# Streaming the high and low token parts of the MLP's first product in one pass

## The chip, the cores and the metric

The kernel runs on one core of a Trainium2 chip. The metric is the device time of one execution in microseconds (us), as the median over runs. The engines are TensorE (PE, with its weight load PEld as a row of its own), VectorE (DVE), ScalarE (ACT), GpSimd (POOL) and SyncE (SP), which issues nearly all the DMAs.

## The reference

A trunk of two decoder layers works on 256 tokens of width 1024 in float32. In each layer one input projection feeds two attention mixers, an output projection adds their result to the residual stream, and a squared-ReLU MLP of width 4096 follows:

```python
for l in range(DEPTH):                       # DEPTH = 2
    h = _rms_norm(x, attn_norm[l])
    proj = h @ w_in[l]                       # 1024 -> 1720
    ...                                      # two attention groups on the same h
    x = x + mixed @ w_out[l]
    h = _rms_norm(x, mlp_norm[l])
    x = x + jnp.square(jax.nn.relu(h @ w_ff1[l])) @ w_ff2[l]     # 1024 -> 4096 -> 1024
return _rms_norm(x, final_norm)
```

## The kernel before

Every large product is made of three reduced-precision ones. An operand is split into a high part (the value rounded to the type float32r) and a low part (what is left), and `mm3` (lines 349 to 354) issues high by high (line 352), high by low (line 353) and low by high (line 354) into one accumulator. Low by low is left out.

**Weights** come from DRAM in the order of use, two chunks of 128 rows by 512 columns at a time (a "tile" here). `ask` (lines 314 to 340) issues the load, then two ScalarE casts make the high part (`whi`, line 334) and two subtractions make the low part (`wlo`, line 336). The engine of the subtractions is given by `lo_eng` (line 312): VectorE for the first two tiles and then for the tiles with an odd number in the layer, GpSimd for the others. Six raw and six split buffers exist, and four tiles are asked for ahead of the one in use.

**Tokens** of a layer are normalised by `norm` (line 417): VectorE multiplies by the gain, TensorE transposes four blocks, and `split_into` (line 389) writes the high part with one ScalarE copy and the low part with one VectorE subtraction, each 512 wide.

**The MLP** of a layer runs in four quarters of 1024 features. In a quarter, `up` (line 1060) is called twice (`fb` = 0 and 1) for 512 features each; features stand on the partitions and the 256 tokens stream. A call does two halves of 256 features. A half goes over the 8 chunks of the contraction and, in each, over two blocks of 128 features (`j`); for each of these pairs `mm3` issues three matmuls of 256 columns, with three weight loads. Both blocks of a half share one PSUM bank of the kind `acc`. When a half is done, `squared_relu` (line 1046) takes the bank to SBUF: relu and square on ScalarE give the high part of `u`, square and subtract on VectorE the low part. Then `down` (line 1082) is called twice (`nb` = 0 and 1) with `u` as the stationary operand and 512 columns of weights streaming, three matmuls for each of 8 chunks and two token tiles. For `nb` = 0 it takes the first four chunks of both token tiles first (they need only the `u` of `fb` = 0), then chunks 4 to 7, which need that of `fb` = 1. For the first `up` of a layer the halves alternate after four chunks, since the second four wait for the later half of the normalised tokens.

**PSUM** has 8 banks, named by kind: `acc` 2, `s` 3, `tr` 2, `pv` 1. Outside the MLP, `s` and `pv` serve the attention, and `s` the first projection of layer 0.

**Order of the work.** TensorE and SP run in the order in which the program's generators are stepped by `Driver`, a planner with a clock of its own; `dr.put` and `dr.event` give it the times at which a bank or a result is taken to be there. The order on VectorE, ScalarE and GpSimd is set by the scheduler of the tile framework. Each engine executes its own list strictly in order.

**The start of the program.** Layer 0's first projection (`proj_both`, PSUM kind `s`) takes the first four tiles of weights, the second projection tiles 5 to 8. Both need the tokens in two halves of 512 features; the second half of the second token tile is the last to be split. Line 1171 makes a small bfloat16 copy of the causal mask (`maskb`) that the attention uses later.

Of the kernel before, what the change touches and what calls it, by code (L numbers as in the profile page):

```python
# [17 lines left out]
L = 2  # L18
# [208 lines left out]
def trunk(ctx: ExitStack, tc: tile.TileContext, x, wst, gains, pos, cw2, cst, out):  # L227
# [83 lines left out]
    def lo_eng():  # L311
        return "v" if at_w[1] <= 2 or at_w[1] % (len(PLAN) // L) % 2 == 1 else "g"
# [104 lines left out]
    def norm(t, nb, g, hT, tag):  # L417

        yield "event", ("x", t, tag, nb * 512)
        if hT[nb] is None:  # L420
            hT[nb] = halves_pair(f"h{nb}")
        h = tm.tile([P, 512], F32, name="h", tag="tm")
        n = slice(nb * 512, nb * 512 + 512)
        with urgent():
            nc.vector.tensor_mul(h, X[t][:, n], g[:, n])
        yield "pe", 0, 700
        c = slice(t * P, (t + 1) * P)
        yield from split_into([h[:, j * P : (j + 1) * P] for j in range(4)], *(x[:, :, c] for x in hT[nb]))
        dr.event(("h", t, tag, nb), 1105)
# [28 lines left out]
    def layer(l, hT):  # L458
# [487 lines left out]
        for ch, r in enumerate(weights(16)):  # L946
# [10 lines left out]
            yield "pe", 300, 0  # L957
# [89 lines left out]
        def squared_relu(acc, u, half):  # L1047

            r = tm.tile([P, 512], F32, name="relu", tag="tm")
            c = slice(half * 2, half * 2 + 2)  # L1050
            hi, lo = (x[:, c, :].rearrange("p c n -> p (c n)") for x in u)
            with urgent():
                nc.scalar.activation(r, acc, AF.Relu)  # L1053
                dr.put("acc", 750)
                nc.scalar.activation(hi, r, AF.Square)
                sq = tm.tile([P, 512], F32, name="sq", tag="tm")
                nc.vector.tensor_mul(sq, r, r)  # L1057
                nc.vector.tensor_sub(lo, sq, hi.bitcast(F32))

        def up(u, fb, first):  # L1060


            src, w, accs, fresh = weights(KC), [], [None, None], [True, True]
            for half, chunks in [(0, (0, 4)), (1, (0, 4)), (0, (4, 8)), (1, (4, 8))] if first else [(0, (0, 8)), (1, (0, 8))]:
                for c in range(*chunks):
# [5 lines left out]
                    if c == 0:  # L1071
                        yield "get", "acc"
                        accs[half] = PS("acc")
                    for j in range(2):
                        f = slice((half * 2 + j) * P, (half * 2 + j + 1) * P)
                        mm3(accs[half][:, j * S : (j + 1) * S], [x[:, f] for x in w[c]], [x[:, c % 4, :] for x in hM[c // 4]], c == 0 and j == 0, c == KC - 1, skip_group_check=True)
                    yield "pe", 6 * 119, 0
                if chunks[1] == KC:
                    squared_relu(accs[half], u[fb], half)
            ev("u", id(u), fb, after=2400)  # L1080
# [66 lines left out]
    def main():  # L1147
# [23 lines left out]
        nc.vector.tensor_copy(maskb, K("causal"))  # L1171
# [27 lines left out]
```

## Time and profile before

| | |
|---|---|
| median of 3 runs (lowest to highest) | 642.43 us (640.5 to 645.75) |
| the profiled execution's own time | 646.11 us |
| its span, first to last instruction | 644.3 us |
| mean granted clock of TensorE | 0.986 |
| busy: PE | 621.4 us, 96% of the span |
| busy: PEld | 548.3 us, 85% |
| busy: DVE | 420.4 us, 65% |
| busy: ACT | 354.6 us, 55% |
| busy: POOL | 300.4 us, 47% |
| DMA | 108.48 MB, mean 168 GB/s |
| chain that ended last | PE 85%, DVE 7%, ACT 4%, DMA 3%, issue 1% |

The profile shows one execution; its time is 3.7 us over the median of the runs. A matmul's busy time runs from its start to the end of its pipeline, and consecutive matmuls overlap, so that the rate of TensorE is read from the distance between starts. A granted clock of 1.00 is 2.4 GHz, 0.50 is 1.2 GHz. "Idle before" is the time in which an engine waited, with the instruction that released it.

### The profile page before, as it was taken

Reading aid. Unit: us, or ns where it says so; the run is one execution under the profiler, and the core shown is the slowest. Engines: PE = TensorE matmul, PEld = TensorE weight load, DVE = VectorE, ACT = ScalarE, POOL = GpSimd, SP = SyncE. Lnnn points to the kernel's source line nnn. Section 1 sums busy time; section 2 is a strip of 40 time slices with the busy share of each in tenths; the row PEclk is TensorE's granted clock in tenths of the full one; section 3 lists DMA queues with packets and bytes.
Section 4 is the critical chain, followed back from the end, with each engine's and each line's share of the span. In section 5 each row is a group of like instructions: output and inputs, shape, how many; then the busy total and the mean of one; then the engine's idle time right before and its main releaser. Section 6 shows DMA issues by size and latency. Waiting matters only on the chain.

```text
span 644.3 us, 10909 instructions
## 1 busy us (share of the span) xinstructions
PE 621.4 (96%) x4099; PEld 548.3 (85%) x4099; DVE 420.4 (65%) x665; ACT 354.6 (55%) x735; POOL 300.4 (47%) x298
## 2 busy tenths in 40 slices
PE   7899899999999999999999889999999999999995
PEld 4697688889889899899888768798998998998985
DVE  4797778675656647558677866866664673764662
ACT  5566667565535546355564475765663654554551
POOL 2675404344553645445466631244544554554351
PEclk8899999999999999999999898999999999999998
DMA  8756733155555655745644665114547565565601
GB/s 306 264 175 206 236 116 100 34 198 173 185 169 191 208 182 166 226 155 186 213 126 134 211 212 199 34 66 149 177 142 220 164 200 174 193 204 176 198 1 66
DMA packets 31732, 108.48 MB, mean 168 GB/s; under 512 B 3776, under 2 KB 4416, under 8 KB 31680
## 3 DMA queue, kind: packets, MB, share of 16 engines
q1 hardware_dynamic: 31392, 107.27, 50.8%
q8 instruction: 32, 0.52, 0.3%
q10 hardware_dynamic: 288, 0.52, 0.2%
q14 instruction: 20, 0.16, 0.1%
HBM read 106.73 MB, written 1.05 MB: 167 GB/s over the span
## 4 chain that ended last, share of the span: by engine, by line
PE 85%; DVE 7%; ACT 4%; DMA 3%; issue 1%; SPq 0%; POOL 0%; POOLq 0%; ACTq 0%
PE acc L352 24%; PE acc L354 24%; PE acc L353 24%; PE tr L384 4%; DVE wlo L336 2%; PE pv L708 2%; DMA raw<-in_wst_dram 2%; PE pv L759 2%; ACT whi L334 1%; PE acc L949 1%; PE s L693 1%; DMA x<-in_x_dram 1%; PE s L746 1%; ACT p L646 1%; DVE qmT L233 1%
## 5 line engine op out<-in xcount | busy, mean ns | idle before, releaser
L336 POOL TENSOR_TENSOR wlo<-raw,whi 128x512 fp32r<-128x512 f32 (+3 forms) x178 | 245.0, 1397 | 221.2 <-ACT whi L334 220.9
L334 ACT CAST whi<-raw 128x512 fp32r<-128x512 f32 (+2 forms) x360 | 201.4, 610 | 113.6 <-PE acc L354 74.7
L336 DVE TENSOR_TENSOR wlo<-raw,whi 128x512 fp32r<-128x512 f32 (+3 forms) x182 | 170.5, 973 | 58.4 <-ACT whi L334 58.3
L352 PE MATMUL acc<-h,whi 128*128 128x256 f32 x512 | 145.3, 284 | 0.0
L354 PE MATMUL acc<-h,wlo 128*128 128x256 f32 x512 | 145.0, 283 | 0.0
L353 PE MATMUL acc<-h,whi 128*128 128x256 f32 x512 | 145.0, 283 | 0.0
L352 PE MATMUL acc<-whi,u 128*128 128x512 f32 (+1 forms) x264 | 101.5, 384 | 0.0
L353 PE MATMUL acc<-wlo,u 128*128 128x512 f32 (+1 forms) x264 | 101.2, 383 | 0.0
L354 PE MATMUL acc<-whi,u 128*128 128x512 f32 (+1 forms) x264 | 101.1, 383 | 0.0
L352 PEld LDWEIGHTS acc<-h,whi 128*128 128x128 f32 x512 | 98.3, 192 | 0.2
L353 PEld LDWEIGHTS acc<-h,whi 128*128 128x128 f32 x512 | 98.3, 192 | 0.2
L354 PEld LDWEIGHTS acc<-h,wlo 128*128 128x128 f32 x512 | 98.3, 192 | 0.0
L1057 DVE TENSOR_TENSOR sq<-relu 128x512 f32<-128x512 f32 x32 | 37.2, 1161 | 38.9 <-ACT relu L1053 38.9
L354 PEld LDWEIGHTS acc<-whi,u 128*128 128x128 f32 x264 | 49.6, 188 | 9.8
L353 PEld LDWEIGHTS acc<-wlo,u 128*128 128x128 f32 x264 | 49.7, 188 | 9.4
L352 PEld LDWEIGHTS acc<-whi,u 128*128 128x128 f32 x264 | 49.7, 188 | 9.3
L1029 DVE SCALAR_TENSOR_TENSOR x<-acc,r,x 128x512 f32<-128x512 f32 (+1 forms) x33 | 24.1, 731 | 49.0 <-PE acc L354 49.0
L1053 ACT ACTIVATE relu<-acc 128x512 f32<-128x512 f32 x32 | 19.0, 594 | 59.3 <-PE acc L354 59.3
L352 PE MATMUL acc<-whi,h 128*128 128x512 f32 (+2 forms) x112 | 41.2, 368 | 0.0
L353 PE MATMUL acc<-wlo,h 128*128 128x512 f32 (+2 forms) x112 | 40.2, 359 | 0.2 <-POOL wlo L336 0.2
L354 PE MATMUL acc<-whi,h 128*128 128x512 f32 (+2 forms) x112 | 39.9, 357 | 0.0
L646 ACT ACTIVATE p<-s,nm 128x128 f32<-128x128 f32 (+1 forms) x96 | 33.9, 430 | 7.9 <-DVE nm L640 4.0
(185 smaller groups left out, 913.3 us busy)
## 6 DMA issues: line engine op xcount, KB each, us to landing
raw<-in_wst_dram SPq DMA_DIRECT2D x178, 512.0 KB, 4.2
raw<-in_wst_dram SPq DMA_DIRECT2D x8, 416.0 KB, 3.3
raw<-in_wst_dram SPq DMA_DIRECT2D x4, 420.0 KB, 3.3
raw<-in_wst_dram SPq DMA_DIRECT2D x4, 384.0 KB, 3.1
x<-in_x_dram SPq DMA_DIRECT2D x4, 256.0 KB, 6.3
g_mix<-in_gains_dram SPq DMA_DIRECT2D x2, 512.0 KB, 5.8
g_mlp<-in_gains_dram SPq DMA_DIRECT2D x2, 512.0 KB, 5.1
g_attn<-in_gains_dram SPq DMA_DIRECT2D x2, 512.0 KB, 3.9
```

The source lines that it names most:

```text
L334: nc.scalar.copy(hi[:, v], r[:, v])
L336: E(eng).tensor_sub(lo[:, v], r[:, v], hi[:, v].bitcast(F32))
L352: mm(acc, ah, wh, start=start, stop=False, **k)
L353: mm(acc, ah, wl, start=False, stop=False, **k)
L354: mm(acc, al, wh, start=False, stop=stop, **k)
L384: nc.tensor.transpose(tr[:rows, c, :], col, ident)
L646: nc.scalar.activation(p[:, k], s[:, k], AF.Exp, bias=nm[:, a : a + 1], scale=scale)
L708: mm(o[:, a, br, :], pts[a // per][:, ((a % per) * 2 + br) * nk + kt, :], V[:, kt, br, g, :], start=kt == 0, stop=kt == nk - 1)
L759: mm(o[:, r, :], pts[r // per][:, (r % per) * nk + kt, :], VM[:, kt, hb * 4 + r, :], start=kt == 0, stop=kt == nk - 1)
L1029: nc.vector.scalar_tensor_tensor(X[t][:, c], acc, scale, X[t][:, c], op0=OP.mult, op1=OP.add)
L1053: nc.scalar.activation(r, acc, AF.Relu)
L1057: nc.vector.tensor_mul(sq, r, r)
```

## The change

In the MLP the normalised tokens are stored as chunk by (high, low) by 256 tokens, so that a chunk's high and low parts lie side by side. For each pair of chunk and feature block, `up` now issues two matmuls: the weights' high part with 512 columns (tokens high and low), which fill a whole bank, and the weights' low part with the 256 high columns, added to the first half of that bank. So each block of 128 features has a bank of its own; a half takes two, (`s`, `s`) for the first half and (`s`, `pv`) for the second. `squared_relu` first adds the two halves of each bank: ScalarE copies columns 256 to 511 to SBUF, VectorE adds columns 0 to 255 to them; then one VectorE instruction gives max(r, 0) times r, ScalarE copies that as the high part of `u`, and VectorE subtracts for the low part. `norm` writes the MLP's tokens with two ScalarE copies and two VectorE subtractions of 256 each instead of one and one of 512. The planner's times are changed with it.

Apart from the MLP, the low parts of the first eight tiles of weights of layer 0 (not only the first two) are made on VectorE, and `maskb` is copied by ScalarE instead of VectorE. One further edit puts a `yield` under `if True:` and does nothing; it is left out here.

```diff
     def lo_eng():
-        return "v" if at_w[1] <= 2 or at_w[1] % (len(PLAN) // L) % 2 == 1 else "g"
+        return "v" if at_w[1] <= 8 or at_w[1] % (len(PLAN) // L) % 2 == 1 else "g"
...
     def norm(t, nb, g, hT, tag):
...
-        if hT[nb] is None:
+        if tag[1] == "mlp":
+            if hT[nb] is None:
+                hT[nb] = [hl.tile([P, 2, 2, S], F32R, name=f"hm{nb}{i}", tag="hl") for i in range(2)]
+        elif hT[nb] is None:
             hT[nb] = halves_pair(f"h{nb}")
...
-        yield from split_into([h[:, j * P : (j + 1) * P] for j in range(4)], *(x[:, :, c] for x in hT[nb]))
+        cols = [h[:, j * P : (j + 1) * P] for j in range(4)]
+        if tag[1] == "mlp":
+
+            tr = yield from trans(cols)
+            with urgent():
+                for i, x in enumerate(hT[nb]):
+                    nc.scalar.copy(x[:, :, 0, c], tr[:, 2 * i : 2 * i + 2, :])
+                    nc.vector.tensor_sub(x[:, :, 1, c], tr[:, 2 * i : 2 * i + 2, :], x[:, :, 0, c].bitcast(F32))
+            dr.put("tr", 1050)
+        else:
+            yield from split_into(cols, *(x[:, :, c] for x in hT[nb]))
...
-        def squared_relu(acc, u, half):
+        def squared_relu(banks, kinds, u, half):
+
 
             r = tm.tile([P, 512], F32, name="relu", tag="tm")
+            low = tm.tile([P, 512], F32, name="sq", tag="tm")
             c = slice(half * 2, half * 2 + 2)
             hi, lo = (x[:, c, :].rearrange("p c n -> p (c n)") for x in u)
             with urgent():
-                nc.scalar.activation(r, acc, AF.Relu)
-                dr.put("acc", 750)
-                nc.scalar.activation(hi, r, AF.Square)
-                sq = tm.tile([P, 512], F32, name="sq", tag="tm")
-                nc.vector.tensor_mul(sq, r, r)
+                for j, acc in enumerate(banks):
+                    n = slice(j * S, (j + 1) * S)
+                    nc.scalar.copy(low[:, n], acc[:, S:])
+                    nc.vector.tensor_add(r[:, n], acc[:, :S], low[:, n])
+                    dr.put(kinds[j], 1000 + 400 * j)
+                sq = low
+                nc.vector.scalar_tensor_tensor(sq, r, 0.0, r, op0=OP.max, op1=OP.mult)
+                nc.scalar.copy(hi, sq)
                 nc.vector.tensor_sub(lo, sq, hi.bitcast(F32))
...
         def up(u, fb, first):
...
+                kinds = (("s", "s"), ("s", "pv"))[half]
...
-                        yield "get", "acc"
-                        accs[half] = PS("acc")
+                        accs[half] = []
+                        for kind in kinds:
+                            yield "get", kind
+                            accs[half].append(PS(kind))
+                    h = hM[c // 4][c % 4 // 2][:, c % 2]
                     for j in range(2):
                         f = slice((half * 2 + j) * P, (half * 2 + j + 1) * P)
-                        mm3(accs[half][:, j * S : (j + 1) * S], [x[:, f] for x in w[c]], [x[:, c % 4, :] for x in hM[c // 4]], c == 0 and j == 0, c == KC - 1, skip_group_check=True)
-                    yield "pe", 6 * 119, 0
+                        wh, wl = w[c]
+                        mm(accs[half][j], wh[:, f], h.rearrange("p k n -> p (k n)"), start=c == 0, stop=False)
+                        mm(accs[half][j][:, :S], wl[:, f], h[:, 0], start=False, stop=c == KC - 1)
+                    yield "pe", 2 * (227 + 120), 0
                 if chunks[1] == KC:
-                    squared_relu(accs[half], u[fb], half)
-            ev("u", id(u), fb, after=2400)
+                    squared_relu(accs[half], kinds, u[fb], half)
+            ev("u", id(u), fb, after=2900)
...
-        nc.vector.tensor_copy(maskb, K("causal"))
+        nc.scalar.copy(maskb, K("causal"))
```

How the lists of the engines move is shown at three places.

On VectorE near the start of the program, before (h is the tokens' low part, wlo the weights'):

```order
L394 TENSOR_TENSOR h_242<-tr,h_241 128x4x128
L336 TENSOR_TENSOR wlo<-raw,whi 128x512 x2
L1171 CAST maskb<-cs 128x128
L394 TENSOR_TENSOR h_242<-tr,h_241 128x4x128
L336 TENSOR_TENSOR wlo<-raw,whi 128x512
L446 SCALAR_TENSOR_TENSOR ra<-s,rx,cs 128x128
```

And with the change:

```order
L394 TENSOR_TENSOR h_242<-tr,h_241 128x4x128
L336 TENSOR_TENSOR wlo<-raw,whi 128x512 x4
L394 TENSOR_TENSOR h_242<-tr,h_241 128x4x128
L336 TENSOR_TENSOR wlo<-raw,whi 128x512 x3
L459 SCALAR_TENSOR_TENSOR ra<-s,rx,cs 128x128
L462 SCALAR_TENSOR_TENSOR rb<-s,rx,cs 128x2x32 x2
L336 TENSOR_TENSOR wlo<-raw,whi 128x512
```

Between the two subtractions of the tokens there are now four subtractions for weights where there were two and the mask; three more follow where there was one, and GpSimd's list loses its first six subtractions.

On TensorE in the MLP's first product, a pair of chunk and feature block and the transposes of the last token half, before (h_1710 holds the tokens' high part, h_1711 their low part):

```order
L352 MATMUL acc<-h_1710,whi 128x256
L353 MATMUL acc<-h_1711,whi 128x256
L354 MATMUL acc<-h_1710,wlo 128x256
L384 MATMUL tr<-idt,h 128x128 x4
L352 MATMUL acc<-h_1710,whi 128x256
```

And with the change (hm is the tile that holds high and low tokens):

```order
L1100 MATMUL s<-hm_1710,whi 128x512
L1101 MATMUL s<-hm_1710,wlo 128x256
L1100 MATMUL pv<-hm_1710,whi 128x512
L1101 MATMUL pv<-hm_1710,wlo 128x256
L384 MATMUL tr<-idt,h 128x128 x4
```

A pair has gone from three matmuls of 256 columns to one of 512 and one of 256, and each of the two pairs shown writes a bank of its own. The transposes of the last token half, which stood behind 24 matmuls of the first `up`, now stand behind 20, which are ten pairs instead of eight.

On VectorE at the end of a quarter's second `up`, before (first and second half, then the weights for `down`):

```order
L1057 TENSOR_TENSOR sq<-relu 128x512
L1058 TENSOR_TENSOR u_2281<-sq,u_2280 128x512
L336 TENSOR_TENSOR wlo<-raw,whi 128x512 x4
L1057 TENSOR_TENSOR sq<-relu 128x512
L1058 TENSOR_TENSOR u_2281<-sq,u_2280 128x512
L336 TENSOR_TENSOR wlo<-raw,whi 128x512 x2
```

And with the change:

```order
L1072 TENSOR_TENSOR relu<-s,sq 128x256 x2
L1075 SCALAR_TENSOR_TENSOR sq<-relu 128x512
L336 TENSOR_TENSOR wlo<-raw,whi 128x512 x2
L1077 TENSOR_TENSOR u_2241<-sq,u_2240 128x512
L336 TENSOR_TENSOR wlo<-raw,whi 128x512 x2
L1072 TENSOR_TENSOR relu<-s,sq 128x256
L1072 TENSOR_TENSOR relu<-pv,sq 128x256
L1075 SCALAR_TENSOR_TENSOR sq<-relu 128x512
L1077 TENSOR_TENSOR u_2241<-sq,u_2240 128x512
L336 TENSOR_TENSOR wlo<-raw,whi 128x512 x2
```

On ScalarE at the same place, before and then with the change:

```order
L1053 ACTIVATE relu<-acc 128x512
L1055 ACTIVATE u_2280<-relu 128x512
L334 CAST whi<-raw 128x512 x8
L1053 ACTIVATE relu<-acc 128x512
L1055 ACTIVATE u_2280<-relu 128x512
L334 CAST whi<-raw 128x512 x16
```

```order
L1071 COPY sq<-s 128x256 x2
L334 CAST whi<-raw 128x512 x2
L1076 CAST u_2240<-sq 128x512
L334 CAST whi<-raw 128x512 x4
L1071 COPY sq<-s 128x256
L334 CAST whi<-raw 128x512 x2
L1071 COPY sq<-pv 128x256
L1076 CAST u_2240<-sq 128x512
L334 CAST whi<-raw 128x512 x16
```

Two additions have come in on VectorE for each half, and the subtraction of the weights' tiles stays where it was for the last half. On ScalarE the last of the four tiles' casts now stands between the two copies of the last half; the number of casts ahead of its end is the same, eight.

## Rows read from the trace of the kernel before

**Rows 1.** Windows by stage: busy time of each engine (instructions), then granted clock, DMA

```profile
28.00:58.00 30.00, 28.73 (x165) 25.73 (x163) 27.28 (x57) 16.86 (x43) 21.45 (x28) 1.00 0.59 193
...
180.00:250.00 70.00, 70.00 (x465) 64.72 (x464) 41.29 (x42) 34.48 (x60) 34.92 (x26) 1.00 0.57 185
```

**Rows 2.** Groups by line: the high-by-low matmuls of the first product

```profile
L353 PE MATMUL acc<-h,whi 128*128 128x256 f32 x512 | 145.0, 283 | 0.0
```

**Rows 3.** Timeline of PE in a quarter: start, us; second product first and last, first product

```profile
167.02 0.40 PE L352 MATMUL acc<-whi,u 128*128 128x512 f32 x1
...
188.58 0.39 PE L354 MATMUL acc<-whi,u 128*128 128x512 f32 x1
188.81 0.28 PE L352 MATMUL acc<-h,whi 128*128 128x256 f32 x1
...
211.72 0.28 PE L354 MATMUL acc<-h,wlo 128*128 128x256 f32 x1
```

**Rows 4.** Lines with 256-wide reads of PSUM on DVE and ACT: min/median/max ns

```profile
L496 DVE TENSOR_TENSOR kT<-tr,kT x8: 406/417/425, 37.0 to 365.1; 128x256 fp32r<-128x256 f32 x8
...
L501 ACT COPY kcT<-tr x4: 362/376/378, 35.9 to 344.7; 128x256 f32<-128x256 f32 x4
```

**Rows 5.** Timeline of DVE at the start of the program

```profile
18.34 2.55 DVE L336 TENSOR_TENSOR wlo<-raw,whi 128x512 fp32r<-128x512 f32 x2 [0.86 <-ACT whi L334]
20.82 1.28 DVE L1171 CAST maskb<-cs 128x128 bf16<-128x128 f32 x1
22.02 0.68 DVE L394 TENSOR_TENSOR h<-tr,h 128x512 fp32r<-128x512 f32 x1
...
26.81 0.35 DVE L446 SCALAR_TENSOR_TENSOR ra<-s,rx,cs 128x128 f32<-128x128 f32 x1 [3.01 <-PE s L354]
```

**Rows 6.** Timelines of ACT and POOL at the same time

```profile
16.65 2.18 ACT L334 CAST whi<-raw 128x512 fp32r<-128x512 f32 x4
18.73 0.58 ACT L393 CAST h<-tr 128x512 fp32r<-128x512 f32 x1
...
17.36 8.82 POOL L336 TENSOR_TENSOR wlo<-raw,whi 128x512 fp32r<-128x512 f32 x6 [0.88 <-ACT whi L334]
```

**Rows 7.** Timeline of PE at the same time, and its next wait

```profile
19.71 0.40 PE L353 MATMUL s<-wlo,h 128*128 128x512 f32 x1
22.76 0.80 PE L354 MATMUL s<-whi,h 128*128 128x512 f32 x1 [2.65 <-DVE h L394]
...
25.84 0.39 PE L352 MATMUL s<-whi,h 128*128 128x512 f32 x1
...
53.78 0.44 PE L384 MATMUL tr<-idt,kd 128*128 128x128 f32 x2 [1.27 <-DVE qT L530]
```

**Rows 8.** Windows behind these two waits (columns as in the first group)

```profile
22.70:25.50 2.80, 2.74 (x7) 2.17 (x8) 1.10 (x1) 0.00 (x0) 2.80 (x3) 0.50 0.96 340
...
53.80:57.00 3.20, 3.20 (x18) 3.15 (x19) 2.21 (x7) 1.54 (x5) 2.29 (x5) 1.00 0.82 270
```

**Rows 9.** Timelines of DVE, ACT and PE at the end of a quarter's first product

```profile
166.31 3.46 DVE L336 TENSOR_TENSOR wlo<-raw,whi 128x512 fp32r<-128x512 f32 x2 [1.53 <-ACT whi L334]
169.69 1.77 DVE L1057 TENSOR_TENSOR sq<-relu 128x512 f32<-128x512 f32 x1
171.57 0.69 DVE L1058 TENSOR_TENSOR u<-sq,u 128x512 fp32r<-128x512 f32 x1
...
167.14 1.14 ACT L334 CAST whi<-raw 128x512 fp32r<-128x512 f32 x2 [0.34 <-issue]
...
174.30 0.39 PE L354 MATMUL acc<-whi,u 128*128 128x512 f32 x1
```

**Rows 10.** Timelines of PE, ACT and DVE at the start of a layer's first product

```profile
143.48 0.36 PE L352 MATMUL acc<-h,whi 128*128 128x256 f32 x1
...
148.38 1.14 ACT L334 CAST whi<-raw 128x512 fp32r<-128x512 f32 x2 [0.73 <-PE acc L353]
...
149.03 1.29 DVE L336 TENSOR_TENSOR wlo<-raw,whi 128x512 fp32r<-128x512 f32 x2 [0.66 <-ACT whi L334]
```

More of the change, by code (lines that the diff above doesn't have):

```diff
@@ L956, in layer @@
                 )
-            yield "pe", 300, 0
+            if True:
+                yield "pe", 300, 0
         dr.spawn(1, hidden_chain(hid))
@@ L1052, in squared_relu @@
             with urgent():
-                nc.scalar.activation(r, acc, AF.Relu)
-                dr.put("acc", 750)
-                nc.scalar.activation(hi, r, AF.Square)
-                sq = tm.tile([P, 512], F32, name="sq", tag="tm")
-                nc.vector.tensor_mul(sq, r, r)
+                for j, acc in enumerate(banks):
[6 more added lines that the diff above has]
+                nc.scalar.copy(hi, sq)
                 nc.vector.tensor_sub(lo, sq, hi.bitcast(F32))
         def up(u, fb, first):
-            src, w, accs, fresh = weights(KC), [], [None, None], [True, True]
+            src, w, accs = weights(KC), [], [None, None]
             for half, chunks in [(0, (0, 4)), (1, (0, 4)), (0, (4, 8)), (1, (4, 8))] if first else [(0, (0, 8)), (1, (0, 8))]:
+                kinds = (("s", "s"), ("s", "pv"))[half]
                 for c in range(*chunks):
```

## The prediction

> **What bounds the kernel now.** I read the windows by stage first. In the MLP, TensorE is busy all the time (70.00 of 70 us between 180 and 250 us) at a granted clock of 1.00, while VectorE works 41.29 us, ScalarE 34.48 and GpSimd 34.92 [rows 1]. So in the MLP a microsecond is won only by giving TensorE less to do, and lost only by making it wait. From 28 to 58 us two engines are nearly full: TensorE 28.73 us of 30, VectorE 27.28 [rows 1].
>
> A matmul's busy time overlaps with the next one's, so the cost of one is read from the distance of starts. In a quarter the first product's 192 matmuls start from 188.81 to 211.72: 191 steps in 22.91 us, 0.1199 us for 256 columns. The second product's 96 start from 167.02 to 188.58: 95 steps in 21.56 us, 0.2269 us for 512 columns [rows 3]. At the clock's upper level (2.4 GHz) 256 columns stream in 0.1067 us and 512 in 0.2133 us, so each matmul with its weight load has some 13 ns on top, at both widths. That is what a wider pass can save.
>
> The timelines of the start show the other place. TensorE issues a matmul at 19.71 and the next, due 0.23 us later, starts at 22.76: it waited for VectorE's low part of the last tokens [rows 7]. VectorE had put two weight subtractions (2.55 us) and the mask copy (1.28 us) ahead of it [rows 5]. GpSimd was subtracting at the time (8.82 us for six) [rows 6]; the same pair takes 1.29 us when it is not [rows 10]. Behind the wait the granted clock is 0.50 (1.2 GHz) for seven matmuls [rows 8], and full speed is back at 25.84 [rows 7].
>
> **The first product.** It has 512 pairs of chunk and feature block, as many as the group of high-by-low matmuls has members [rows 2]. A pair is three passes of 0.1199 us, 0.3597, and becomes 0.2269 + 0.1199 = 0.3468: 0.0129 us less, 6.6 us over 512 pairs. TensorE is the bound throughout these stretches, so all of it counts.
>
> The price of a 512-column pass is taken from the second product, where it streams weights and not tokens; the width, the type and the bank that it fills are the same. By "TensorE: Matmul & The Clock Gate" of the Trainium skill, section "Back-to-back issue gap", a warm gap is N/2.4 + 2.5 ns, so that joining two passes would save 2.5 ns, an estimate of 1.3 us over 512 pairs. The rows here are 13 ns over the streaming time, and I go by them.
>
> **Emptying the banks.** Each half gains two additions of 256 out of PSUM on VectorE. The nearest row is a 256-wide subtraction that reads PSUM, 0.42 us; the copies on ScalarE are as a 256-wide copy, 0.38 us [rows 4]. That is 0.84 us on VectorE for each of 32 halves (27 us), with the max-times instruction in the place of the multiplication; ScalarE gains some 0.1 us a half, since two copies and a cast replace relu and square. The stretch of 70 us holds about six halves: VectorE goes from 41.3 to about 46.5 us in it. There is room, and weights are asked for four tiles ahead.
>
> Where it could reach TensorE is the end of a quarter's second `up`. The second product needs the last low part at 174.30, 7.28 us after it began; VectorE has it at 171.57 + 0.69 = 172.26, 2.04 us early [rows 3, 9]. I follow the new list. VectorE is with the weights until 169.69, as before. ScalarE's copies are there by then: the pair of casts at 167.14 moves back by one copy and ends at 168.7, the second copy at 169.0. The two additions end at 170.5. The max-times instruction takes 0.69 us (as the subtraction) to 1.77 us (as the multiplication beside GpSimd) [rows 9], so 171.2 to 172.3; the cast adds 0.6 and the subtraction 0.69: 172.5 to 173.6. That is 0.7 to 1.8 us early. Cost 0, hidden by the second product's first 30 matmuls.
>
> The tokens' low parts at a layer's start come in two halves; 0.84 us instead of 0.69 on VectorE. The later half's second cast stands behind a weight pair on ScalarE that waits for TensorE to free a buffer and ends at 149.52; VectorE's pair ends at 150.32 [rows 10], the second half then at about 150.7. TensorE starts at 143.48 [rows 10] and needs it after 20 pairs (6.9 us) and four transposes (about 0.4 us): at 150.8. It just fits: I take 0. Should GpSimd run beside VectorE's pair, that takes 3.46 us instead of 1.29 [rows 9], and TensorE would wait about 2 us in each layer: 0 to 4 us. In the rows GpSimd isn't running there, so 0.
>
> Banks: `s` and `pv` are idle in the MLP, a half's two are used again only after the other half (5.5 us), and `down` keeps `acc` to itself. Cost 0.
>
> **The start.** Now GpSimd has no subtractions there. VectorE does four for the weights after its first token part, two pairs of 1.29 us from about 17.4, since the casts come in the same 2.18 us from 16.65 [rows 6]: until about 19.9. The last tokens' cast ends at 19.31 [rows 6], their subtraction (0.68 us) at about 20.6. TensorE, due at 19.94, goes on at about 20.65 instead of 22.76: 2.1 us. Its wait shrinks to 0.7 us. Behind a wait of 1.27 us at 53.78 the granted clock stayed at 1.00 [rows 7, 8], so I expect full speed here: the seven slow matmuls took 25.84 - 22.76 = 3.08 us and would take 7 x 0.227 = 1.59, another 1.5 us. TensorE is then 3.6 us ahead.
>
> How much of it reaches the end is decided by VectorE, for which TensorE next waits (53.78) [rows 7]. VectorE's first work on the projection waits for TensorE at 26.81 [rows 5] and moves up by 3.6 us too, but behind it two more weight subtractions now lie (of the six moved, the other four go ahead of it): 1.3 us. So VectorE is 2.3 us ahead if it never idles from there on, and up to 3.6 if its gaps (2.7 us in 28 to 58 [rows 1]) take the 1.3. Bounds: 0.8 us (the clock falls all the same, 2.1 - 1.3) and 4.3 us (no wait at all is left, 2.8 + 1.5). I take 3.2, nearer the upper middle, since part of the gaps are waits for casts that TensorE releases. The mask's copy costs ScalarE 0.3 us, hidden in front of its long idle time while VectorE waits at 26.81. Behind this stretch, no list changes until the MLP, so the lead is handed on.
>
> **Sum.** 6.6 + 3.2 = 9.8 us. The profiled execution took 646.11 us and would take 636.3. It lies 3.7 us over the median, 642.43, from which the forecast follows: **632.6 us**.
>
> **Rivals.**
> - *The start's lead is used up*: the clock falls behind the shorter wait as well, and VectorE, nearly full from 28 to 58 us, keeps its 1.3 us. For it speaks how full it is [rows 1]; against it the wait of 1.27 us that left the clock alone. 6.6 + 0.8 = 7.4: 635.0 us.
> - *A 512-column pass between 256-column ones is not as cheap as in a row of its own*: if it takes 0.237 us, as two passes of 256 would but for 2.5 ns, only 1.3 us is won. Against it stands that the 13 ns are the same at both widths [rows 3]. 1.3 + 3.2 = 4.5: 637.9 us. It is what the page's formula named above would give.
> - *Slower: TensorE waits for the last low part in each quarter.* If ScalarE's pair of casts, now between the last half's two copies, must wait for a buffer that the second product frees (after about 18 matmuls, 4.1 us, at 171.1), then casts 1.14, copy 0.38, addition 0.42, max-times 1.77, cast 0.6 and subtraction 0.69 end at 176.1, 1.8 us late; eight quarters make 14.4 us: 647.0 us. It decides from 9.8 / 8 = 1.2 us of waiting in a quarter. Against it: that pair ran at 167.14 without waiting for TensorE [rows 9], and as many casts stand ahead of the half's end as before.
>
> **How the numbers follow.** The forecast has 65 in 100, its own range 630 to 635.5; the lost lead 22; the dear pass 6; the waits in the quarters 4; 3 are left for what I don't see. The range should leave out the last two and part of the third: 628.5, for a start that gains all of its 4.3 us and a median that scatters as the runs before do (640.5 to 645.75), up to 638. Faster by over 1% (below 636.0; about what a measurement of this kernel tells from no change) are nearly all of the first case and over half of the second: 75. Within 1%: 22. Slower by over 1%: 3.
>
> **What would show it.** In the first product, starts that alternate at 0.227 and 0.120 us, and a quarter's two `up` in about 22.2 us instead of 23.0. At the start, TensorE's wait for the tokens' low part below 1 us and no window at 0.50 behind it; the matmul that started at 25.84 at about 22.2; the MLP of layer 0 beginning about 3 us earlier than 143.48. No waits of TensorE for `u` or hm in the MLP. Wrong would be: the 512-column pass at over 0.235 us, a lead that is gone by 58 us, or a wait at the seventh matmul group of the second product in each quarter.

## The result and the profile after

The changed kernel takes 634.23 us (633.68 to 635.02, four runs) where the kernel before takes 641.46 (640.1 to 645.75): a ratio of 0.9858, interval 0.9811 to 0.9904, so 1.4% faster. Here and below a ratio and its interval are estimated over the executions, without those over 1.5% above their kernel's fastest, and are not the quotient of the medians beside them (here 0.9887, or 7.2 us). The forecast of 632.6 us lies 1.6 us below, the range holds it. But two of the terms behind it did not come out, as the rows show. The profiled execution after took 635.02 us, with a span of 633.2 and a mean granted clock of 0.995.

The windows by stage of the changed kernel (columns: stretch, then PE, PEld, DVE, ACT, POOL busy with instructions, clock, DMA share, GB/s) answer [rows 1]; the first and last are of the start and of layer 1's attention:

```profile
0.00:28.00 28.00, 25.15 (x99) 17.07 (x100) 19.45 (x39) 17.65 (x36) 6.77 (x18) 1.00 0.91 325
28.00:58.00 30.00, 29.75 (x224) 25.62 (x223) 27.78 (x57) 19.34 (x54) 21.19 (x29) 1.00 0.62 200
180.00:250.00 70.00, 70.00 (x366) 59.68 (x366) 44.37 (x60) 38.25 (x75) 37.47 (x25) 1.00 0.56 183
318.00:447.00 129.00, 124.67 (x862) 106.22 (x861) 94.73 (x207) 77.47 (x191) 59.69 (x74) 0.99 0.46 149
```

In the MLP stretch TensorE is still busy all the time; VectorE went from 41.29 to 44.37 us. From 28 to 58 us TensorE is now full as well (29.75).

The timeline of PE of the changed kernel (start, busy us, engine, line, operation; in brackets the wait and its releaser), at the start and in a quarter, answers [rows 3] and [rows 7]:

```profile
18.47 0.40 PE L353 MATMUL s<-wlo,h 128*128 128x512 f32 x1
19.31 0.50 PE L354 MATMUL s<-whi,h 128*128 128x512 f32 x1 [0.44 <-DVE h L394]
...
161.85 0.40 PE L352 MATMUL acc<-whi,u 128*128 128x512 f32 x1
...
183.67 0.39 PE L1100 MATMUL s<-hm,whi 128*128 128x512 f32 x1
...
185.31 0.28 PE L1101 MATMUL s<-hm,wlo 128*128 128x256 f32 x1
185.42 0.40 PE L1100 MATMUL s<-hm,whi 128*128 128x512 f32 x1
185.66 0.28 PE L1101 MATMUL s<-hm,wlo 128*128 128x256 f32 x1
185.78 0.40 PE L1100 MATMUL s<-hm,whi 128*128 128x512 f32 x1
...
206.27 0.40 PE L352 MATMUL acc<-whi,u 128*128 128x512 f32 x1
```

Two things are to be seen. The wait at the start is 0.44 us instead of 2.65. And in the first product the step from a 512-column pass to the next start is 0.24 us, the other 0.11: over the trace the means of the rows are 0.2360 us (508 steps) and 0.1172 (502), from starts given to 0.01 us. From 183.67 to 206.27 are 64 pairs in 22.60 us, 0.353 a pair, where the forecast had 0.3468 and the kernel before 0.3597.

Where the time went, from the starts of the first matmul of each stage in the two profiled executions (the MLP of layer 0 is taken to end at the first matmul behind the last transposes ahead of layer 1's projection, 322.74 and 316.26 us, that of layer 1 at the last matmul):

| stretch (us) | before | after | change |
|---|---|---|---|
| program start to the first projection's first matmul | 10.28 | 9.47 | -0.81 |
| from there to the attention's first product with its table (FT) | 49.71 | 45.01 | -4.70 |
| from there to the MLP of layer 0 | 83.49 | 83.55 | +0.06 |
| MLP of layer 0, with its end | 179.26 | 178.23 | -1.03 |
| attention of layer 1 | 134.74 | 131.14 | -3.60 |
| MLP of layer 1 | 179.98 | 178.99 | -0.99 |

The first line lies ahead of all changed work. The attention of layer 1 holds no changed work either. The MLP gave 2.0 us, less than forecast, and the start 4.7 in this pair, more than forecast.

### The profile page after: what moved, and what is told of

It reads as the page before. It is cut to its first block, busy times and chain, and to the rows that moved or that the text cites. A ratio compares the mean times of both kernels' runs of the same rounds, so it can differ in the third digit from the quotient of the medians.

```text
span 633.2 us, 9990 instructions
## 1 busy us (share of the span) xinstructions
PE 615.3 (97%) x3587; PEld 518.7 (82%) x3587; DVE 424.0 (67%) x742; ACT 354.6 (56%) x776; POOL 305.8 (48%) x292
## 4 chain that ended last, share of the span: by engine, by line
PE 83%; DVE 9%; ACT 3%; DMA 2%; issue 2%; POOL 0%; POOLq 0%; SPq 0%; ACTq 0%; DVEq 0%
PE acc L352 14%; PE acc L353 14%; PE acc L354 14%; PE s L1100 14%; PE s L1101 7%; PE pv L1100 5%; PE tr L384 4%; DVE wlo L336 3%; PE pv L1101 2%; PE pv L721 2%; DMA raw<-in_wst_dram 2%; PE pv L772 2%; DVE h L428 1%; PE acc L962 1%; ACT whi L334 1%
## 5 line engine op out<-in xcount | busy, mean ns | idle before, releaser
L336 POOL TENSOR_TENSOR wlo<-raw,whi 128x512 fp32r<-128x512 f32 (+3 forms) x172 | 249.2, 1472 | 208.8 <-ACT whi L334 208.4
L336 DVE TENSOR_TENSOR wlo<-raw,whi 128x512 fp32r<-128x512 f32 (+3 forms) x188 | 162.1, 899 | 53.5 <-ACT whi L334 53.5
L1100 PE MATMUL s<-hm,whi 128*128 128x512 f32 x384 | 141.7, 399 | 0.0
L1101 PE MATMUL s<-hm,wlo 128*128 128x256 f32 x384 | 107.8, 281 | 0.0
L1100 PEld LDWEIGHTS s<-hm,whi 128*128 128x128 f32 x384 | 72.2, 188 | 17.8
L1101 PEld LDWEIGHTS s<-hm,wlo 128*128 128x128 f32 x384 | 72.5, 189 | 0.2
L1100 PE MATMUL pv<-hm,whi 128*128 128x512 f32 x128 | 51.0, 399 | 0.0
L1071 ACT COPY sq<-s 128x256 f32<-128x256 f32 x48 | 17.6, 372 | 39.2 <-PE s L1101 38.6
L1076 ACT CAST u<-sq 128x512 fp32r<-128x512 f32 x32 | 19.8, 619 | 31.2 <-DVE sq L1075 31.2
L1101 PE MATMUL pv<-hm,wlo 128*128 128x256 f32 x128 | 36.0, 281 | 0.0
```

What stands on the lines that cost most here:

```text
L336: E(eng).tensor_sub(lo[:, v], r[:, v], hi[:, v].bitcast(F32))
L1071: nc.scalar.copy(low[:, n], acc[:, S:])
L1076: nc.scalar.copy(hi, sq)
L1100: mm(accs[half][j], wh[:, f], h.rearrange("p k n -> p (k n)"), start=c == 0, stop=False)
L1101: mm(accs[half][j][:, :S], wl[:, f], h[:, 0], start=False, stop=c == KC - 1)
```

## The experiments

### The two halves of the change, apart

One kernel takes the MLP of the change and leaves the start as it was, the other the reverse.

```diff
 # the MLP alone, against the changed kernel
-        return "v" if at_w[1] <= 8 or ...
+        return "v" if at_w[1] <= 2 or ...
-        nc.scalar.copy(maskb, K("causal"))
+        nc.vector.tensor_copy(maskb, K("causal"))
```

> The MLP's part alone: the start as before (low parts of the third, fifth ... tile on GpSimd, the mask's copy on VectorE). By the sizes of the prediction (a pair of passes at 0.347 us instead of 0.360) it is 6.6 us faster than before. By the trace of the changed kernel (0.353 us a pair, and some 0.7 us lost at each layer's first product) it is 2.0 us faster, and its starts in the first product stand 0.236 and 0.117 us apart.

Measured: 640.07 us (12 runs) against 645.56 (23 runs), ratio 0.9959, interval 0.9919 to 0.9999: about 2.6 us. (The tiles whose low parts stay on GpSimd here are the fourth, sixth and eighth, not the third and fifth.)

```diff
 # the start alone, against the kernel before
-        return "v" if at_w[1] <= 2 or ...
+        return "v" if at_w[1] <= 8 or ...
-        nc.vector.tensor_copy(maskb, K("causal"))
+        nc.scalar.copy(maskb, K("causal"))
```

> The start's part alone: the first eight tiles' low parts on VectorE and the mask's copy on ScalarE, the MLP as before. By the sizes of the prediction 3.2 us faster than before. By the trace of the changed kernel 4.6 us faster, most of it from a wait below 0.7 us for the tokens' low part and no stretch at a granted clock of 0.50 behind it. If the clock of the start is chance and not made by that wait, about 2 us.

Measured: 639.82 us (12 runs) against the same 645.56, ratio 0.9924, interval 0.989 to 0.9957: about 4.9 us. The two intervals overlap and the two medians lie 0.25 us apart, so these times alone don't say which half is larger. Part of the scatter goes with the clock: among the executions of this series with a mean granted clock of 0.989 or more the medians are 641.2 us before (8), 639.3 with the MLP alone (9) and 638.2 with the start alone (8), so 1.9 and 2.9 us. The traces say the same (2.0 us for the MLP, 2.9 to 3.3 for the start, below). So the start is the larger half, the MLP the smaller, the reverse of my sum.

In the trace of the MLP alone a quarter is 22.60 us again, as in the changed kernel. The wait at the start stands there in full (timeline of PE of the MLP alone):

```profile
19.27 0.40 PE L353 MATMUL s<-wlo,h 128*128 128x512 f32 x1
22.32 0.50 PE L354 MATMUL s<-whi,h 128*128 128x512 f32 x1 [2.65 <-DVE h L394]
22.66 0.40 PE L352 MATMUL s<-whi,h 128*128 128x512 f32 x1
22.89 0.39 PE L353 MATMUL s<-wlo,h 128*128 128x512 f32 x1
```

A wait of 2.65 us, as long as in [rows 7], and yet the matmuls behind it follow at 0.23 us, at the clock's upper level (a granted clock of 1.00 from 22.30 to 25.10 us). The half clock of [rows 8] is not tied to this wait: it came in one execution and not in another.

### Why a pair costs 0.353 us: three theories

A: the 256-column pass adds to columns that the pass just ahead of it has written, and has to wait for them. B: a change of width from one pass to the next costs something. C: the change of bank from pair to pair costs it.

The first test lets the 256 columns go to the other half of the bank; the sum is the same, since the halves are added later.

```diff
-                        mm(accs[half][j][:, :S], wl[:, f], h[:, 0], start=False, stop=c == KC - 1)
+                        mm(accs[half][j][:, S:], wl[:, f], h[:, 0], start=False, stop=c == KC - 1)
```

> The changed kernel with the 256-column pass added to columns 256 to 511 of the bank instead of 0 to 255 (the two are added afterwards, so the sum is the same). Theory A: the narrow pass is held because it adds to columns that the wide pass has just written; columns 256 to 511 are written later, so the wide start to the narrow one grows from 0.236 us to 0.25 or more. Theory B: what costs is a narrow pass behind a wide one, wherever it writes: 0.236 and 0.117 stay. Theory C: the change of bank costs: they stay too.

Measured: steps of 0.2361 and 0.1171 us (636.22 us, one execution). Nothing changes, but this is no full test of A, since the 512-column pass writes both halves.

The second puts the two 512-column passes of a chunk first and then the two of 256.

```diff
-                    for j in range(2):
-                        ...
-                        mm(accs[half][j], wh[:, f], h.rearrange("p k n -> p (k n)"), ...)
-                        mm(accs[half][j][:, :S], wl[:, f], h[:, 0], ...)
+                    for j, f in enumerate(fs):
+                        mm(accs[half][j], wh[:, f], h.rearrange("p k n -> p (k n)"), ...)
+                    for j, f in enumerate(fs):
+                        mm(accs[half][j][:, :S], wl[:, f], h[:, 0], ...)
```

> The changed kernel with the passes of a chunk's two feature blocks in the order wide, wide, narrow, narrow, so that each narrow pass adds to a bank that was written two passes ago. The four take 0.707 us in the changed kernel. Theory A (a bank just written): the extra goes, 0.694 us, some 3.4 us less over the MLP. Theory B (a narrow pass behind a wide one): one such step instead of two, 0.700 us. Theory C (a change of bank): four changes instead of two, 0.720 us.

Measured: a quarter's two `up` from 183.11 to 205.40, 22.29 us, 0.6966 us for two pairs (630.82 us, one execution). The uniform streams give 0.694 us and the changed kernel 0.706, so three quarters of the loss come back. It lies between what was expected by A (0.694) and by B (0.700) and decides nothing between them.

The third streams 512 columns in both passes. It computes more than the reference: the low by low product is added too.

```diff
-                        mm(accs[half][j][:, :S], wl[:, f], h[:, 0], ...)
+                        mm(accs[half][j], wl[:, f], h.rearrange("p k n -> p (k n)"), ...)
```

> The changed kernel with the weights' low part streaming the tokens' high and low parts too, so that all passes of the first product are 512 wide (it adds low by low, more work: 512 passes of 256 columns). Theories A (a bank just written) and B (a step between widths) as before. If neither a new bank nor the tokens as streaming operand costs, the starts stand 0.227 us apart as in the second product, 0.454 a pair, and the kernel takes about 52 us longer. If a wide pass of tokens is dearer by itself, 0.234 to 0.236 us each.

The timeline of PE of this kernel in the first product:

```profile
190.94 0.39 PE L1100 MATMUL s<-hm,whi 128*128 128x512 f32 x1
191.17 0.39 PE L1101 MATMUL s<-hm,wlo 128*128 128x512 f32 x1
191.40 0.39 PE L1100 MATMUL s<-hm,whi 128*128 128x512 f32 x1
```

The steps are 0.2268 us, although tokens stream and every second pass adds to the columns of the one ahead (689.08 us, for the added work). So the price that I took from the second product holds for tokens too, as long as all passes are of one width. That speaks against A and for B.

The fourth stays in one bank for two chunks, so that the bank changes half as often (cuts stand as "...", here and in the next diffs).

```diff
+                        for cc in (c - 1, c):
+                            ...
-                        mm(accs[half][j], wh[:, f], h.rearrange(...), start=c == 0, stop=False)
-                        mm(accs[half][j][:, :S], wl[:, f], h[:, 0], start=False, stop=c == KC - 1)
+                            mm(accs[half][j], wh[:, f], h.rearrange(...), start=cc == 0, stop=False)
+                            mm(accs[half][j][:, :S], wl[:, f], h[:, 0], start=False, stop=cc == KC - 1)
```

> The changed kernel with two chunks in a row for one feature block: wide, narrow, wide, narrow into one bank, then four into the other. The change of bank comes half as often, the step between widths and the bank just written as often as in the changed kernel. Theory C (change of bank): a pair goes from 0.353 to 0.350 us. Theories A and B: 0.353 stays; if A holds for wide passes too, 0.356.

Measured: 0.236 and 0.1172 us, so C falls (637.45 us, one execution; TensorE waits 0.78 us for hm in each layer's first `up`, since two chunks at a time need the tokens sooner).

The fifth keeps the widths alternating, but the 256-column pass is never that of the bank written just before it: wide of block 0, narrow of block 1 for the chunk before, wide of block 1, narrow of block 0.

```diff
+                    mm(accs[half][0], wh[:, fs[0]], h.rearrange(...), start=c == 0, stop=False)
+                    if c > chunks[0]:
+                        narrow(1, c - 1)
+                    mm(accs[half][1], wh[:, fs[1]], h.rearrange(...), start=c == 0, stop=False)
+                    narrow(0, c)
+                    ...
```

> The changed kernel with the narrow passes one step later: wide to bank 0, narrow to bank 1 (chunk before), wide to bank 1, narrow to bank 0. Widths alternate as in the changed kernel, but a narrow pass never follows the wide pass of its own bank (a wide one follows the narrow one of its own bank). Theory A (a wide pass, then a narrow one to the same bank): the extra goes, 0.348 us a pair as in the order wide, wide, narrow, narrow. Theory B (alternating widths): 0.353 us stays.

Measured: a quarter's `up` from 183.55 to 206.14, 22.59 us, as with the change (22.60), and 634.24 us. So A falls as it was put, for narrow passes. Every wide pass here follows the narrow pass of its own bank; that a wide pass waiting for it isn't the price either is shown by the fourth test: there three of four passes follow one of their own bank instead of two, and the steps stay at 0.236 and 0.117 us. Of the three theories B is left, the alternation of widths.

### Longer runs of one width

If each change of width costs the same, runs of four should be better still than runs of two. I timed both together with the kernel before. The first is the order "wide, wide, narrow, narrow" of above, the second takes two chunks at a time outside the first `up` of a layer:

```diff
+                    group = [c] if first else [c - 1, c]
+                    ...
+                    for cc in group:
+                        ...
+                        for j, f in enumerate(fs):
+                            mm(accs[half][j], w[cc][0][:, f], h.rearrange(...), ...)
+                    for cc in group:
+                        for j, f in enumerate(fs):
+                            mm(accs[half][j][:, :S], w[cc][1][:, f], h[:, 0], ...)
```

> The order wide, wide, narrow, narrow once more, timed in rounds. A pair took 0.348 us there instead of 0.353, which is 0.3 us in each of eight quarters: by that it is 2.5 us faster than the changed kernel, and with its 1.4% (0.9858) at a ratio of about 0.982 to the kernel before.

> Four wide passes and then four narrow ones (two chunks by two feature blocks), except in a layer's first call. Theory B (a step between widths costs 6.4 us per thousand steps): a quarter of the steps of the changed kernel, 0.3484 us a pair; if the cost falls faster than the number of steps, as wide, wide, narrow, narrow suggests (a quarter of the cost at half of the steps), 0.347 us, another 0.5 us or less for the whole kernel than that order.

Runs of two: 632.59 us (630.17 to 636.23, six runs) against 643.0, ratio 0.9837, interval 0.9793 to 0.9881. Runs of four: 634.26 us (631.24 to 635.28, six), ratio 0.9852, interval 0.9807 to 0.9897. The two kernels can't be told apart by their times, nor either from the changed kernel; the traces can tell them. First the timeline of PE with runs of two, in which the profile puts equal neighbours into one row:

```profile
187.99 0.63 PE L1100 MATMUL s<-hm,whi 128*128 128x512 f32 x2
188.46 0.39 PE L1102 MATMUL s<-hm,wlo 128*128 128x256 f32 x2
188.68 0.40 PE L1100 MATMUL s<-hm,whi 128*128 128x512 f32 x1
```

And with runs of four:

```profile
187.76 1.09 PE L1104 MATMUL s<-hm,whi 128*128 128x512 f32 x4
188.69 0.64 PE L1108 MATMUL s<-hm,wlo 128*128 128x256 f32 x4
189.17 1.09 PE L1104 MATMUL s<-hm,whi 128*128 128x512 f32 x4
```

Two wide passes take 0.47 us and two narrow 0.22, together 0.69; four wide take 0.93 (0.233 each, not 0.227) and four narrow 0.48. By the quarter: 22.29 us with runs of two (184.51 to 206.80), 22.43 with runs of four (184.98 to 207.41), 22.60 alternating. So runs of four are better than alternation, but dearer than runs of two. "Each change of width costs the same" is too simple: the wide passes are dearer wherever narrow ones are mixed in, the narrow ones somewhat cheaper. No run varied the weight load that goes with each pass, so whether that has a part in it, and what in TensorE makes this, stays open.

### What made the start faster

The kernel before was profiled a second time, and the two edits of the start were made one at a time.

> The kernel before once more, for a second profile. If the long stretch of layer 1's attention (the compressed branch's product to the next step 22.8 us, in the changed kernel 19.5) belongs to the kernel, it is there again; if it was chance in one execution, it is near 19.5 us, and the start is as in the first profile: a wait of 2.65 us and a granted clock of 0.50 behind it.

```diff
 # the mask alone, against the kernel before
-        nc.vector.tensor_copy(maskb, K("causal"))
+        nc.scalar.copy(maskb, K("causal"))
```

> The kernel before with the mask's copy on ScalarE, nothing else. The copy took 1.28 us ahead of the tokens' low part, in an execution with a wait of 2.65 us, while GpSimd was subtracting. If the copy is what matters, TensorE's wait falls to 0.3 to 1.4 us and the second projection starts about 1.3 us earlier after the first than before (15.1 to 17.6 us).

```diff
 # the low parts alone, against the kernel before
-        return "v" if at_w[1] <= 2 or ...
+        return "v" if at_w[1] <= 8 or ...
```

> The kernel before with the low parts of the first eight tiles on VectorE, the mask's copy still there. If it is GpSimd's subtractions beside VectorE's that make the wait, the copy is short then (0.3 us or less) and the wait 0.7 to 0.8 us; the second projection starts 13.9 us after the first (13.6 in the changed kernel). If the two more subtractions ahead of the tokens' part cost what the engine gains, the wait stays near 2 us.

Measured, one execution each: before again 638.53 us, the mask alone 642.44, the low parts alone 637.76. The second profile of the kernel before does not repeat the start of the first: the wait is 1.58 us, and the granted clock behind it 1.00 (20.60 to 23.40 us). The whole times scatter too much to be read; the stretch from the first projection to FT doesn't:

| kernel | TensorE's wait for the last tokens | first projection to FT |
|---|---|---|
| before | 2.65 | 49.71 |
| before again | 1.58 | 48.43 |
| MLP alone (start as before) | 2.65 | 47.91 |
| mask alone | 1.45 | 48.12 |
| low parts alone | 0.58 | 45.13 |
| both (start alone) | 0.44 | 44.99 |
| the changed kernel | 0.44 | 45.01 |
| runs of two, runs of four | 0.63, 0.64 | 45.54, 45.71 |

With the low parts moved it is 45.0 to 45.7 us, without them 47.9 to 49.7. Only in the first profile of the kernel before was the clock low for a larger part of this stretch: the mean granted clock is 0.95 in it, in the other rows 0.99 or 1.00. The mask is worth nothing that can be seen here. The reason stands on VectorE. The kernel before, second profile, timeline of DVE:

```profile
17.33 2.54 DVE L336 TENSOR_TENSOR wlo<-raw,whi 128x512 fp32r<-128x512 f32 x2 [0.68 <-ACT whi L334]
19.79 0.21 DVE L1171 CAST maskb<-cs 128x128 bf16<-128x128 f32 x1
19.93 0.68 DVE L394 TENSOR_TENSOR h<-tr,h 128x512 fp32r<-128x512 f32 x1
```

And the changed kernel, which answers [rows 5]:

```profile
16.16 2.49 DVE L336 TENSOR_TENSOR wlo<-raw,whi 128x512 fp32r<-128x512 f32 x4
18.57 0.69 DVE L394 TENSOR_TENSOR h<-tr,h 128x512 fp32r<-128x512 f32 x1
19.17 1.89 DVE L336 TENSOR_TENSOR wlo<-raw,whi 128x512 fp32r<-128x512 f32 x3
21.98 0.35 DVE L459 SCALAR_TENSOR_TENSOR ra<-s,rx,cs 128x128 f32<-128x128 f32 x1 [0.92 <-issue]
```

Four subtractions without GpSimd beside them take 2.49 us; two with it (GpSimd subtracts from 16.32 to 19.32 in the second profile) take 2.54. So VectorE does the double work in the same time, and without the wait of 0.68 us for ScalarE's casts. The section "SBUF: two separate sides" of the Trainium skill's page "SBUF — State Buffer" says that VectorE and GpSimd share a pair of ports, which one instruction holds as a whole; these rows agree with it. The mask's copy took 0.21 us here and 1.28 in [rows 5].

The low parts also take away two later waits of TensorE. The kernel before, second profile, timeline of PE:

```profile
36.95 0.44 PE L384 MATMUL tr<-idt,kcv 128*128 128x128 f32 x2 [1.45 <-DVE kT L496]
...
51.60 0.44 PE L384 MATMUL tr<-idt,kd 128*128 128x128 f32 x2 [1.08 <-DVE qT L530]
```

The mask alone keeps both (1.55 and 1.08 us); the low parts alone have 0.10 us left of the first and nothing of the second, but 0.17 us at 33.09. From the second projection to FT that is 31.42 us instead of 33.37 (32.09 in the first profile of the kernel before, whose longer wait at the start left only the second of the two).

## Why the prediction was right or wrong

**The first product: direction right, size wrong.** 6.6 us were forecast, 2.0 came. The step that failed is the price of a 512-column pass, "taken from the second product". It was right for a stream of one width, tokens or weights, and wrong next to 256-column passes: 0.2360 + 0.1172 = 0.3532 us instead of 0.3468, so 6.5 ns a pair instead of 12.9, 3.3 us over 512 pairs. My sentence against the dear pass, that "the 13 ns are the same at both widths", argued from two uniform streams to a mixed one, which no row of before showed. A 512-column pass at over 0.235 us was also the first thing that the prediction named as showing it wrong. The rival with 0.237 us for the wide pass had that number right and was given 6 in 100; it missed that the narrow pass becomes cheaper, 0.117 instead of 0.120. By the page's formula (section "Back-to-back issue gap" of "TensorE: Matmul & The Clock Gate" in the Trainium skill, which gives it for an isolated matmul) a pair would save 2.5 ns; the runs show 6.5 alternating and 11.4 in runs of two, so for these passes the rows decide against it.

**A layer's first product: a wait that I did not look for.** Of the 3.3 us the first `up` of each layer gives back 0.7: from 138.03 to 161.85 it takes 23.82 us, before 23.54, where 0.43 less was due. The MLP alone has 23.82 too and the start alone 23.54, so it belongs to the MLP's half of the change. The summary of the changed kernel's waits of PE has no `u` and no hm, as forecast, but this row (us in total, times, longest):

```profile
PE tr L384 <- DVE h L428: 2.1, 3, 1.1
```

One of the three is at the start; the other two are 0.51 us in each layer. The timelines of PE, DVE and POOL of the changed kernel at that place:

```profile
141.53 0.28 PE L1101 MATMUL pv<-hm,wlo 128*128 128x256 f32 x1
142.31 0.63 PE L384 MATMUL tr<-idt,h 128*128 128x128 f32 x4 [0.51 <-DVE h L428]
...
138.12 0.68 DVE L1041 TENSOR_TENSOR x<-acc,x 128x512 f32<-128x512 f32 x1
138.72 1.74 DVE L336 TENSOR_TENSOR wlo<-raw,whi 128x512 fp32r<-128x512 f32 x1
140.39 1.78 DVE L428 TENSOR_TENSOR h<-x,g_mlp 128x512 f32<-128x512 f32 x1
...
138.62 2.99 POOL L336 TENSOR_TENSOR wlo<-raw,whi 128x512 fp32r<-128x512 f32 x2 [1.54 <-ACT whi L334]
```

And those of DVE and POOL of the kernel before at the same place:

```profile
143.80 0.68 DVE L1027 TENSOR_TENSOR x<-acc,x 128x512 f32<-128x512 f32 x1
144.51 1.40 DVE L425 TENSOR_TENSOR h<-x,g_mlp 128x512 f32<-128x512 f32 x1
...
144.07 3.00 POOL L336 TENSOR_TENSOR wlo<-raw,whi 128x512 fp32r<-128x512 f32 x2 [1.88 <-ACT whi L334]
```

Between the residual's addition and the multiplication by the gain VectorE now has a subtraction for the weights, 1.74 us beside GpSimd, and the multiplication itself takes 1.78, where before it stood right behind the addition and took 1.40. TensorE is ready for the transposes at 141.80; VectorE ends at 142.17 and TensorE goes on at 142.31. From the last pass ahead of these transposes to the first behind them it is 1.17 us (141.53 to 142.70), in the kernel before 0.47 (146.31 to 146.78): that is the whole 0.7 us. I had followed the tokens' low parts, one step later in the list, and put GpSimd's presence there at zero; it was there one step earlier, in the kernel before as well. My upper bound for this place was 4 us, and the wait with what stands around it costs 1.4 in all.

**Emptying the banks: right.** VectorE in a quarter's end, which answers [rows 9]:

```profile
161.18 2.46 DVE L336 TENSOR_TENSOR wlo<-raw,whi 128x512 fp32r<-128x512 f32 x2 [0.94 <-ACT whi L334]
163.57 0.41 DVE L1072 TENSOR_TENSOR relu<-s,sq 128x256 f32<-128x256 f32 x1
163.90 0.41 DVE L1072 TENSOR_TENSOR relu<-pv,sq 128x256 f32<-128x256 f32 x1
164.35 1.00 DVE L1075 SCALAR_TENSOR_TENSOR sq<-relu 128x512 f32<-128x512 f32 x1
166.09 0.95 DVE L1077 TENSOR_TENSOR u<-sq,u 128x512 fp32r<-128x512 f32 x1 [0.74 <-ACT u L1076]
```

The additions cost 0.41 us, the max-times instruction 1.00, within 0.69 and 1.77. The last low part is there at 167.04, 5.19 us after the second product began and so 2.1 us early; 0.7 to 1.8 were forecast. VectorE has 44.37 us in the stretch of 70, forecast 46.5. No bank is waited for. The rival with waits in each quarter did not come.

**The start: size about right, by luck, and reasons only in part.** 3.2 us were forecast; the kernels with the low parts moved average 45.3 us to FT (the five above), those without 48.5 (four), so 3.3; without the first profile, the one with the low clock, 48.2 and so 2.9. The wait shrank to 0.44 us (0.7 forecast), and VectorE kept nothing of the lead for itself. But I gave 1.5 us of it to the clock, which was a chance of that one execution, and 1.28 us on the way to the mask, which is 0.21 elsewhere. In their place stand VectorE's subtractions without GpSimd, which were in my sum for this stretch, and the two later waits that vanish, which were not: I feared that two subtractions behind the projection would cost VectorE 1.3 us, and TensorE waits less there instead.

**The total** came near by luck. 9.8 us were forecast; the changed stretches give 2.0 in the MLP, 4.6 short, and 2.9 to 3.3 in the start, together 4.9 to 5.3. Measured are 8.2 us from the median that the forecast stood on (642.43), 7.2 from the later one and 9.1 by the ratio (interval 6.2 to 12.1). So some 2 us or more of the gain I can't put at a place of its own, and they brought the time close to the forecast. The mean clock does not explain them: the executions of the kernel before at 0.989 or more have medians of 641.2 and 641.7 us in the two other series, 7 us above the changed kernel's 634.2. Yet the second profile of the kernel before and the profiled execution of the changed kernel, both at 0.995, lie only 3.5 us apart (638.53 and 635.02). What the change is worth beyond its traced 5 us stays open.

## What to carry to other kernels

A pass's price from a stream of one width does not hold next to passes of another width; order equal widths together, two by two here (22.29 us a quarter instead of 22.60 in the traces; the whole times can't tell these orders apart), and read the price from such a mixture. VectorE's time for an operation with two inputs from SBUF should be taken with and without GpSimd beside it, for moving GpSimd's work to VectorE can cost VectorE nothing (four subtractions alone 2.49 us, two beside GpSimd 2.54). And where a list is reordered, each wait of TensorE's chain has to be followed from its first link, here the multiplication ahead of the transposes.

## What the runs showed of the hardware

- *Widths.* Passes with a weight load each, starts apart: all of 256 columns 0.1199 us, all of 512 0.2268 to 0.2269, alternating 0.2360 and 0.1172; a pair 0.3483 us in runs of two, 0.3505 in runs of four, 0.3532 alternating, 0.3468 as the sum of the uniform prices. Changing the bank half as often (0.236 and 0.117), the columns written before (22.59 and 22.60 us a quarter) and the kind of the streaming operand (0.2268 tokens, 0.2269 weights) made no difference.
- *The clock between executions.* In the 34 executions of the kernel before that were timed in two series, the 15 with a mean granted clock of 0.989 or more took 638.96 to 644.07 us, the 19 with less 644.44 to 651.27. The profiled one had 0.986, and its low places account for most of the 3.6 us that layer 1's attention took longer than in the changed kernel; the windows of the kernel before there:

```profile
325.00:457.00 132.00, 126.21 (x860) 106.76 (x859) 96.90 (x205) 77.50 (x188) 58.69 (x74) 0.97 0.44 144
...
383.00:390.00 7.00, 5.21 (x37) 3.53 (x40) 5.03 (x11) 5.45 (x14) 3.35 (x4) 0.82 0.59 214
```

  Its second profile has 0.99 from 320 to 450 us, and that attention takes 130.65 us, as with the change (131.14). Over all fourteen traces this attention, from its first projection's first matmul, takes 127.6 to 128.2 us where its mean granted clock is 1.00 (three traces), 128.3 to 129.9 at 0.99 (eight), 131.6 and 132.6 at 0.97 and 132.9 at 0.96, whichever MLP or start the kernel has. All four runs of the changed kernel have 0.992 or more. That the change makes low clocks rarer isn't shown: the start alone had 0.981 to 0.995 in its 12 runs. It isn't excluded either: the 12 timed executions of runs of two and of four had 0.991 or more, the 11 of the kernel before beside them 0.981 to 0.996.
